# Layer a's transposed probabilities read back in a step of their own

## The chip, the cores and the metric

The kernel runs on one core of a Trainium2 chip. The metric is the time of one execution on the device in microseconds (us), the median of several runs.

## What is computed

A trunk of two residual layers on 256 tokens of width 2048, 16 heads of 128. Layer a is multi-head latent attention, layer b block-sparse attention with ALiBi (at 256 tokens: causal attention over one block). Cut to what matters for layer a:

```python
def mla_mixer(h, w_in, ...):
    q_lat, kv_lat, k_rope, gate = split(h @ w_in)
    q  = norm(q_lat) @ w_q_up      # per head 128 + 64 (rotary)
    kv = norm(kv_lat) @ w_kv_up    # per head k 128, v 128
    ...                            # RMS norm of q and k, rotary
    p = softmax(causal(q k^T * scale))
    return (p @ v) * silu(gate)
x = x + mla_mixer(rms_norm(x), ...) @ w_out_a
```

## The kernel before

**Matmuls.** A float32 product is made of three fast matmuls: every operand is split into a high part and a low part (`wh`, `wl` for weights, `ph`, `pl` for probabilities, `ohl` for the gated output). For each block of weights (512 KB, tile `wr`), ScalarE (ACT) makes `wh` (line 147), VectorE (DVE) makes `wl` (line 151), and TensorE (PE) uses both. Loads of weights go through SyncE's (SP's) queue, four blocks ahead.

**Layer a by pairs of heads.** `group_a(g)`, g = 0 to 7, does heads 2g and 2g+1, called pair g here. It projects q (`w_q_up`, blocks 384 wide) and k, v (`w_kv_up`, one block 512 wide), norms, and turns q, k and the rotary part by PE transposes in three steps, turn 0, 1, 2 (`ps_ta`; tiles `tok`, `tok`, `ra`), whose results ACT (`sf`, `sr`, lines 421 and 426) and DVE (`sr`, line 427) split. Blocks of the gate projection stand between a pair and the next.

**A head** has three steps (`head_steps`, line 450). `s1`: scores on PE (`ps_s`), then softmax on DVE and ACT, into `sm`. `s2`: the probabilities are transposed by a DMA: `fly` writes the two 16-bit halves of each float32 apart ("planes", line 441, on ACT in layer a) into `pz` and issues a DMA transpose from SP's queue (line 442) into `sm`; `flip` then copies the planes back together on DVE (line 448, `pz<-sm`). Then ACT makes `ph` (line 490) and `p` (line 493, in float32 for the second half) and DVE `pl` (line 491). `s3`: four matmuls with v (`ps_o`), the product with the gate `og` (DVE, line 505), its high part `ohl` (ACT, 506) and low part (DVE, 507).

**What sets the order.** `ordered` lays the main list (projections) and the side list (turns and heads) out on PE's planned time. A step becomes ready `lag * 1.3` ns after the steps that it needs; PE's order is fixed by that. The instructions of DVE, ACT and SP are then ordered by the framework's scheduler, by what becomes ready, each engine working its queue off in order. `head_steps` already has a second form, with `away`: `s2` only sends the planes off, and a further step `s2_back` copies them back (line 483, held at its place in the program by `keep_in_program_order`) and makes `ph`, `pl`, `p`. Layer b uses it (`FLB`, 4500 ns).

**The end of layer a.** The output projection `w_out_a` begins while the last pairs are still at work: four blocks of columns run through heads 0 to 11 first (48 PE steps of 0.67 us each), then through heads 12 to 15. Meanwhile SP reloads `x` (line 772) and layer b's distances into `c_sb` (line 768), from which ACT makes `alibi` (line 883).

Of the kernel before, what the change touches and what calls it, by code (L numbers as in the profile page):

```python
# [44 lines left out]


PA, PB, LO, TU, TUB, S1, S2A, S2B, S3 = 9000, 6000, 5000, 3000, 10000, 4800, 6000, 9000, 3000
FLB = 4500
SLACK = 1.3
HOLD = 4500  # L50
PACE, PACEB = 600, 3500
# [42 lines left out]
def trunk(ctx: ExitStack, tc, xT, gains, cst, w_in_a, w_q_up, w_kv_up, w_out_a, w_in_b, w_out_b, outT):  # L94
    nc = tc.nc
# [560 lines left out]
    def group_a(g):  # L656
# [65 lines left out]
        def scores(h):  # L722
            def f(ps):
                at = lambda x, i: [y[:, i] for y in x]
                products(ps, at(z["q"], h), at(z["k"], h), True)
                products(ps, at(z["r"], 0), at((krf,) + lat_st["kr"], h), False)
            return f
# [5 lines left out]
        for h in range(2):  # L733
            heads.append(head_steps(2 * g + h, scores(h), lambda: c_sb[:, C_MASK:C_MASK + 384],
                                    lambda h=h: [x[:, h] for x in z["v"]], 1090, turns + [kr], [], gates[g][-1:],
                                    S2A, nc.scalar.copy))
        proj[0].needs += lats
        if g > 1:
            proj[-1].after += turns_of[-2]
# [55 lines left out]
    for g in range(8):  # L795
        main += group_a(g)
        if g == 0:
            kr.after.append(main[-1])
        if g < 7:
            main += gates[g + 1][HALF:] + (gates[g + 2][:HALF] if g < 6 else [])  # L800
        gates[g][-1].after.append(row_a)
        if g > 3:
            gates[g][-1].after += [h[2] for h in heads[2 * g - 8:2 * g - 6]]
# [21 lines left out]
    def group_b(g):  # L825
# [49 lines left out]
        def scores(h):  # L875
            def f(ps):
                products(ps, [x[:, h] for x in z["Q"]], [x[:, h] for x in z["K"]], True)
            return f

        def bias(h):  # L880
            def f():
                b = wk.tile([P, 384], F32, tag="alibi", name="alibi", bufs=1)
                nc.scalar.activation(b, c_sb[:, C_MASK:C_MASK + 384], AF.Copy,
                                     scale=float(np.float32(2.0 ** (-8.0 * (h + 1) / H))))
                return b
            return f
# [12 lines left out]
        for h in range(4):  # L899
            hb.append(head_steps(4 * g + h, scores(h), bias(4 * g + h), lambda h=h: [x[:, h] for x in z["v"]],  # L900
                                 545, [tq, tk], v[-1:] + gate[-1:], [], S2B, nc.vector.tensor_copy, PACEB if g < 3 else PACE, FLB))
        for s in (gate[NC - 1], gate[-1]):
# [96 lines left out]
```

## Time and profile before

| | |
|---|---|
| median of 3 runs | 753.29 us (752.79, 753.29, 755.86) |
| profiled execution, its own time | 756.72 us |
| span in its trace | 754.9 us |
| PE, DVE, ACT busy | 99%, 78%, 65% of the span |
| DMA traffic | 153 MB, mean 203 GB/s |

Around the span lie 1.8 us (756.72 - 754.9). The matmuls' ends in a trace are modelled, so a wait of PE is read from the starts of successive matmuls: 256 columns follow one another every 0.11 us, 512 columns every 0.22 us.

### The profile page before, as it was taken

To read this page: it belongs to the slowest core of one execution; us is meant where nothing else is said; L and a number is where in the kernel's file an instruction comes from. 1 tells how busy PE (TensorE), PEld (TensorE's weight loads), DVE (VectorE), ACT (ScalarE), POOL (GpSimd) and SP (SyncE) were. 2 spreads that over 40 slices of the span, in tenths; PEclk is the share of its full clock that TensorE was granted. 3 is DMA by queue.
4 is the path that set the end of the run, shared out by engine and by line. 5 is a ranking of instruction groups with operands and counts; after the bars stand their busy time and mean duration, and the time that the engine had idled before them with its cause. 6 is when DMAs were issued, how large, how long until landed. Compare 5 with 4: busy or idle time off the path is not lost.

```text
span 754.9 us, 13198 instructions
## 1 busy us (share of the span) xinstructions
PE 743.7 (99%) x4766; PEld 692.0 (92%) x4766; DVE 589.7 (78%) x1244; ACT 492.1 (65%) x1041; POOL 0.2 (0%) x4
## 2 busy tenths in 40 slices
PE   8999999999999999999999999999999999999997
PEld 7999999999899999988889988898889988899997
DVE  6978899998898696875888967887787968878563
ACT  7867888887787475555666766666566756665441
POOL 0000000000000000000000000000000000000000
PEclk9999999999999999999999999999999999999999
DMA  9866666666566957667888868777778878767771
GB/s 294 265 182 182 167 184 162 182 172 158 161 195 170 299 172 227 198 191 200 222 230 208 203 195 234 224 195 208 197 235 226 197 204 228 230 197 196 248 223 49
DMA packets 150258, 153.13 MB, mean 203 GB/s; under 512 B 47280, under 2 KB 119344, under 8 KB 150192
## 3 DMA queue, kind: packets, MB, share of 16 engines
q1 hardware_dynamic: 150048, 152.27, 71.5%
q8 instruction: 37, 0.61, 0.3%
q14 instruction: 29, 0.24, 0.1%
q10 hardware_dynamic: 144, 0.02, 0.0%
HBM read 139.68 MB, written 2.10 MB: 188 GB/s over the span
## 4 chain that ended last, share of the span: by engine, by line
PE 89%; DVE 5%; DMA 3%; ACT 1%; issue 1%; SPq 0%; DVEq 0%; ACTq 0%
PE acc L199 82%; PE ps_s L199 4%; DVE wl L151 3%; PE ps_o L199 2%; PE ps_ta L202 1%; DMA c_sb<-cst 1%; DMA sm<-pz 1%; DMA wr<-w_in_a 1%; ACT wh L147 1%; DVE xt L406 0%; ACT sq L598 0%; DVE rs_y L328 0%; DVE rs_t L327 0%; PE ps_lt L202 0%; DVE pl L491 0%
## 5 line engine op out<-in xcount | busy, mean ns | idle before, releaser
L147 ACT ACTIVATE wh<-wr 128x1024 fp32r<-128x1024 f32 (+3 forms) x265 | 288.3, 1092 | 145.6 <-PE acc L199 118.9
L151 DVE TENSOR_TENSOR wl<-wr,wh 128x1024 fp32r<-128x1024 f32 (+3 forms) x265 | 313.9, 1188 | 74.1 <-PE acc L199 42.5
L199 PE MATMUL acc<-wh,xhl 128*128 128x512 f32 (+1 forms) x896 | 266.1, 376 | 1.5 <-ACT wh L147 1.5
L199 PEld LDWEIGHTS acc<-wh,xhl 128*128 128x128 f32 x896 | 169.1, 190 | 22.6 <-ACT wh L147 2.2
L199 PE MATMUL acc<-xhl,wh 128*128 128x256 f32 (+1 forms) x768 | 173.5, 313 | 0.0
L199 PE MATMUL acc<-ohl,wh 128*128 128x256 f32 (+1 forms) x800 | 172.5, 307 | 0.1
L199 PE MATMUL acc<-wl,xhl 128*128 128x512 f32 (+1 forms) x448 | 167.8, 374 | 0.8 <-DVE wl L151 0.8
L199 PE MATMUL acc<-ohl,wl 128*128 128x256 f32 x512 | 140.5, 274 | 0.4 <-DVE wl L151 0.3
L199 PE MATMUL acc<-xhl,wl 128*128 128x256 f32 x512 | 140.2, 274 | 0.0
L199 PEld LDWEIGHTS acc<-ohl,wh 128*128 128x128 f32 x800 | 130.1, 191 | 6.2 <-DVE ohl L507 0.3
L199 PEld LDWEIGHTS acc<-xhl,wh 128*128 128x128 f32 x768 | 126.3, 191 | 6.6
L199 PEld LDWEIGHTS acc<-ohl,wl 128*128 128x128 f32 x512 | 98.3, 192 | 0.9 <-DVE wl L151 0.8
L199 PEld LDWEIGHTS acc<-xhl,wl 128*128 128x128 f32 x512 | 98.2, 192 | 0.2
L199 PEld LDWEIGHTS acc<-wl,xhl 128*128 128x128 f32 x448 | 84.9, 190 | 11.3 <-DVE wl L151 1.3
L199 PE MATMUL acc<-wh,xt 128*128 128x384 f32 (+1 forms) x192 | 58.5, 362 | 0.0
L466 ACT ACTIVATE sm<-sm,mn 128x128 f32<-128x128 f32 x64 | 29.1, 456 | 12.8 <-DVE mn L464 12.8
L199 PEld LDWEIGHTS acc<-wh,xt 128*128 128x128 f32 x192 | 35.6, 192 | 1.4
L199 PE MATMUL acc<-wl,xt 128*128 128x384 f32 (+1 forms) x96 | 34.0, 354 | 2.1 <-DVE wl L151 2.1
L406 DVE TENSOR_TENSOR xt<-acc,xt 128x256 f32<-128x256 f32 (+1 forms) x37 | 16.1, 484 | 14.7 <-PE acc L199 14.7
L490 ACT CAST ph<-pz 128x256 fp32r<-128x256 f32 x32 | 12.9, 404 | 21.0 <-DVE pz L483 10.7
L507 DVE TENSOR_TENSOR ohl<-og,ohl 128x256 fp32r<-128x256 f32 x32 | 13.5, 424 | 12.0 <-ACT ohl L506 11.8
L506 ACT ACTIVATE ohl<-og 128x256 fp32r<-128x256 f32 x32 | 13.8, 435 | 13.5 <-DVE og L505 13.5
(150 smaller groups left out, 726.9 us busy)
## 6 DMA issues: line engine op xcount, KB each, us to landing
wr<-w_in_b SPq DMA_DIRECT2D x128, 512.0 KB, 4.0
wr<-w_in_a SPq DMA_DIRECT2D x32, 512.0 KB, 4.1
wr<-w_out_a SPq DMA_DIRECT2D x32, 512.0 KB, 4.5
wr<-w_out_b SPq DMA_DIRECT2D x32, 512.0 KB, 4.4
wr<-w_in_a SPq DMA_DIRECT2D x15, 416.0 KB, 5.2
wr<-w_q_up SPq DMA_DIRECT2D x16, 384.0 KB, 3.7
wr<-w_kv_up SPq DMA_DIRECT2D x8, 512.0 KB, 3.9
xt<-xT SPq DMA_DIRECT2D x4, 512.0 KB, 5.6
```

The lines of the kernel that those rows point to most:

```text
L147: nc.scalar.activation(self.ordering(self.h)[1], self.ordering(self.raw)[0], AF.Copy)
L151: nc.vector.tensor_tensor(self.ordering(self.l)[1], self.ordering(self.raw)[0], self.ordering(self.h.bitcast(F32))[1], op=ALU.subtract)
L199: chain(nc.tensor.matmul(*args, skip_group_check=True, **kw))
L202: chain(nc.tensor.transpose(*args))
L406: nc.vector.tensor_tensor(lines(y), unpaired(b[:, o:o + n]), lines(y), op=ALU.add)
L466: nc.scalar.activation(sm[:, sl], sm[:, sl], AF.Exp, bias=mn[:, t:t + 1], scale=-1.0, accum_out=rs[:, t:t + 1])
L490: nc.scalar.copy(ph, pz[:, :S])
L506: nc.scalar.activation(lines(ogh[:, h]), unpaired(og), AF.Copy)
L507: nc.vector.tensor_tensor(lines(ogl[:, h]), unpaired(og), lines(ogh[:, h].bitcast(F32)), op=ALU.subtract)
```

## The change

Layer a's heads take the second form: `head_steps` gets `away=FLA`, 4000 ns. The transposes go off in `s2`; the copy back and the making of `ph`, `pl` and `p` are a step of their own, planned 2000 ns (`S2A - FLA`) times 1.3 after that, so the sum of the lags up to `s3` stays 6000 ns times 1.3. The instructions are the same ones; the copy's line is 483 in place of 448.

```diff
-FLB = 4500
+FLA, FLB = 4000, 4500
...
-                                    S2A, nc.scalar.copy))
+                                    S2A, nc.scalar.copy, away=FLA))
```

What this does to the queues, at four places. First DVE, around the products of pair 0's turns (`sr`), before; the two copies and both `pl` stand above these rows:

```order
L394 TENSOR_TENSOR gx<-acc,rr_a 128x512
L491 TENSOR_TENSOR pl<-pz,ph 128x256
L151 TENSOR_TENSOR wl<-wr,wh 128x768
L396 SCALAR_TENSOR_TENSOR gate<-gate,gx 128x512
L427 SCALAR_TENSOR_TENSOR sr_1356<-ps_ta,gq_a,sr_1356 128x256
L427 SCALAR_TENSOR_TENSOR sr_1356<-ps_ta,g_sb,sr_1356 128x512
L427 SCALAR_TENSOR_TENSOR sr_1356<-ps_ta,sr_1356 128x128
L151 TENSOR_TENSOR wl<-wr,wh 128x1024 x2
L505 SCALAR_TENSOR_TENSOR og<-ps_o,gate 128x256
```

And the same place now:

```order
L427 SCALAR_TENSOR_TENSOR sr_1342<-ps_ta,gq_a,sr_1342 128x256
L427 SCALAR_TENSOR_TENSOR sr_1342<-ps_ta,g_sb,sr_1342 128x512
L483 COPY pz<-sm 128x2x384
L151 TENSOR_TENSOR wl<-wr,wh 128x1024
L427 SCALAR_TENSOR_TENSOR sr_1342<-ps_ta,sr_1342 128x128
L483 COPY pz<-sm 128x2x384
L491 TENSOR_TENSOR pl<-pz,ph 128x256
L151 TENSOR_TENSOR wl<-wr,wh 128x1024
L491 TENSOR_TENSOR pl<-pz,ph 128x256
L505 SCALAR_TENSOR_TENSOR og<-ps_o,gate 128x256
```

The first `wl` of 1024 columns here is that of `w_kv_up`. In pair 0 one copy stands ahead of it and both `pl` behind it. In pairs 1 to 4 the first copy stands between the first two `sr`, the first `pl` after the second `sr`, and the second copy and `pl` behind that `wl`, as in pair 2 now:

```order
L427 SCALAR_TENSOR_TENSOR sr_2038<-ps_ta,sr_2038 128x128
L151 TENSOR_TENSOR wl<-wr,wh 128x1024
L483 COPY pz<-sm 128x2x384
L151 TENSOR_TENSOR wl<-wr,wh 128x1024
L491 TENSOR_TENSOR pl<-pz,ph 128x256
L505 SCALAR_TENSOR_TENSOR og<-ps_o,gate 128x256
```

PE's order is the same up to pair 5. There turn 2 of pair 6 (`ra`) now stands ahead of the second head's `ps_o`, where before it came one half of `w_kv_up` later:

```order
L199 MATMUL acc<-wh,xt 128x512
L202 MATMUL ps_ta<-c_sb,ra 128x128 x2
L199 MATMUL ps_o<-ph,vh 128x256
L199 MATMUL ps_o<-pl,vh 128x256
L199 MATMUL ps_o<-ph,vl 128x256
L199 MATMUL ps_o<-p_3147,v_2524 128x128
```

ACT's queue at that place, now; `p_3147` is what the last matmul above reads, and `sf_3089<-ps_ta 128x128` reads turn 2's result. Before, this `ph` and `p` stood ahead of all of pair 6's `sf`:

```order
L668 ACTIVATE sqa,ga_st<-acc 128x64
L421 ACTIVATE sf_3089<-ps_ta 128x128
L666 ACTIVATE sqa,ga_st<-acc 128x128
L490 CAST ph<-pz 128x256
L668 ACTIVATE sqa,ga_st<-acc 128x64
L493 COPY p_3147<-pz 128x128
L666 ACTIVATE sqa,ga_st<-acc 128x128
L506 ACTIVATE ohl<-og 128x256
```

In the last pairs more moves: the scores of pair 6 come four PE steps earlier, its `ps_o` two and four steps earlier, and the two `ps_o` of pair 7 three steps later (after 44 and 48 steps of the output projection, before after 41 and 45). In ACT's queue `alibi` now stands ahead of the last head's `ohl`, before it stood behind it. SP's queue has the same instructions; the transposes of pairs 6 and 7 take other places between the loads.

## Rows read from the trace of the kernel before

**Rows 1.** The page's busy time by engine: busy us, share of the span, instructions.

```profile
PE 743.7 (99%) x4766; PEld 692.0 (92%) x4766; DVE 589.7 (78%) x1244; ACT 492.1 (65%) x1041; POOL 0.2 (0%) x4
```

**Rows 2.** The chain of waits over 80 to 260 us, in order of time: start us, length us, what. Shown are the second head's scores that follow pairs 2, 3 and 4, one piece on DVE, and the chain's end in the reload of `c_sb`.

```profile
152.71 1.16 PE ps_s L199 x10
...
168.72 1.14 DVE wl L151
...
174.98 1.16 PE ps_s L199 x10
...
200.66 1.16 PE ps_s L199 x10
...
255.65 7.74 DMA c_sb<-cst
```

**Rows 3.** PE's timeline in pair 3, around the two halves of `w_kv_up` (columns: start us, us, engine, line, operation, in brackets idle time before it and its releaser).

```profile
169.25 0.49 PE L199 MATMUL acc<-wh,xt 128*128 128x512 f32 x1
169.91 0.48 PE L199 MATMUL acc<-wl,xt 128*128 128x512 f32 x1 [0.17 <-DVE wl L151]
170.23 0.59 PE L199 MATMUL acc<-wh,xt 128*128 128x512 f32 x2
...
171.20 0.28 PE L199 MATMUL ps_o<-pl,vh 128*128 128x256 f32 x1
...
171.59 0.49 PE L199 MATMUL acc<-wh,xt 128*128 128x512 f32 x1
171.91 0.38 PE L199 MATMUL acc<-wl,xt 128*128 128x512 f32 x1
```

**Rows 4.** DVE's timeline in pair 3, from the second copy to the `wl` of `w_kv_up`.

```profile
165.49 0.61 DVE L448 COPY pz<-sm 128x768 uint16<-128x768 uint16 x1 [0.16 <-DMA sm<-pz]
...
166.62 0.42 DVE L491 TENSOR_TENSOR pl<-pz,ph 128x256 fp32r<-128x256 f32 x1
166.96 0.48 DVE L427 SCALAR_TENSOR_TENSOR sr<-ps_ta,gq_a,sr 128x256 fp32r<-128x256 f32 x1
167.77 0.75 DVE L427 SCALAR_TENSOR_TENSOR sr<-ps_ta,g_sb,sr 128x512 fp32r<-128x512 f32 x1 [0.33 <-ACT sr L426]
168.44 0.28 DVE L427 SCALAR_TENSOR_TENSOR sr<-ps_ta,sr 128x128 fp32r<-128x128 f32 x1
168.64 2.35 DVE L151 TENSOR_TENSOR wl<-wr,wh 128x1024 fp32r<-128x1024 f32 x2
```

**Rows 5.** Pair 4: DVE's second copy, from its timeline.

```profile
189.55 0.61 DVE L448 COPY pz<-sm 128x768 uint16<-128x768 uint16 x1 [1.97 <-DMA sm<-pz]
```

**Rows 6.** Pair 4: PE's timeline.

```profile
191.65 0.35 PE L199 MATMUL ps_o<-ph,vh 128*128 128x256 f32 x1 [0.47 <-DVE sr L427]
...
193.97 0.65 PE L199 MATMUL acc<-wl,xt 128*128 128x512 f32 x1 [1.26 <-DVE wl L151]
```

**Rows 7.** Busy time by stretch, 190 to 194 us and 194 to 198 us: length, PE, PEld, DVE, ACT, POOL busy (instructions), granted clock of PE as a share of full speed, DMA share, GB/s.

```profile
190.00:194.00 4.00, 2.27 (x15) 1.68 (x13) 3.67 (x8) 3.73 (x12) 0.00 (x0) 1.00 0.29 102
194.00:198.00 4.00, 4.00 (x13) 3.45 (x14) 2.31 (x5) 3.00 (x15) 0.00 (x0) 0.57 0.59 189
```

**Rows 8.** Pair 0: PE's timeline.

```profile
101.92 0.28 PE L199 MATMUL ps_o<-pl,vh 128*128 128x256 f32 x1
...
102.31 0.49 PE L199 MATMUL acc<-wh,xt 128*128 128x512 f32 x1
103.07 0.48 PE L199 MATMUL acc<-wl,xt 128*128 128x512 f32 x1 [0.27 <-DVE wl L151]
```

**Rows 9.** Pair 0: DVE's timeline, from the first copy to the second `sr`.

```profile
95.27 0.60 DVE L448 COPY pz<-sm 128x768 uint16<-128x768 uint16 x1
...
98.88 0.95 DVE L151 TENSOR_TENSOR wl<-wr,wh 128x768 fp32r<-128x768 f32 x1
99.75 0.69 DVE L396 SCALAR_TENSOR_TENSOR gate<-gate,gx 128x512 f32<-128x512 f32 x1
```

**Rows 10.** Pair 5: ACT's timeline, the second head's `ph` and `p`, an `sqa`, and the first `ohl`.

```profile
213.15 0.41 ACT L490 CAST ph<-pz 128x256 fp32r<-128x256 f32 x1
213.46 0.29 ACT L493 COPY p<-pz 128x128 f32<-128x128 f32 x1
...
215.31 0.29 ACT L666 ACTIVATE sqa<-acc 128x128 f32<-128x128 f32 x1
...
215.56 1.08 ACT L147 ACTIVATE wh<-wr 128x1024 fp32r<-128x1024 f32 x1
```

**Rows 11.** Pair 5: PE's timeline, the second head's `ps_o` and, later, turn 2.

```profile
216.38 0.27 PE L199 MATMUL ps_o<-ph,vh 128*128 128x256 f32 x1
...
218.28 0.38 PE L202 MATMUL ps_ta<-c_sb,ra 128*128 128x128 f32 x2
```

**Rows 12.** The end of layer a on ACT: the last head's `ohl` and `alibi`.

```profile
259.41 0.43 ACT L506 ACTIVATE ohl<-og 128x256 fp32r<-128x256 f32 x1
263.42 0.52 ACT L883 ACTIVATE alibi<-c_sb 128x384 f32<-128x384 f32 x1 [3.58 <-DMA c_sb<-cst]
```

**Rows 13.** The end of layer a on PE: two late `wl`.

```profile
252.22 0.39 PE L199 MATMUL acc<-ohl,wh 128*128 128x256 f32 x2
252.65 0.38 PE L199 MATMUL acc<-ohl,wl 128*128 128x256 f32 x1
...
275.79 0.38 PE L199 MATMUL acc<-ohl,wl 128*128 128x256 f32 x1 [0.31 <-DVE wl L151]
```

## The prediction

> **What bounds the kernel now.** First the page's busy time: PE is busy for 743.7 of 754.9 us, DVE 78%, ACT 65% [rows 1]. So nearly all of the time is matmuls that the change leaves as they are, and it can only win back or add waits of PE. Next the chain of waits over layer a [rows 2]: it runs on PE, with one piece of 1.14 us on DVE in each pair, the `wl` of `w_kv_up`. The reader should then look at PE's timeline there [rows 3]: the matmul with `wl` starts 0.66 us after the one with `wh` (169.25 to 169.91), while the same step half a block later takes 0.32 (171.59 to 171.91). That is 0.34 lost, and the next matmul loses 0.10 more (0.32 instead of 0.22): 0.45 us a pair.
>
> DVE's timeline says why `wl` is late [rows 4]. Ahead of it in DVE's queue stand the second head's copy, which waits 0.16 for its DMA, and its `pl`, and an `sr` that waits 0.33 for ACT. In pair 4 the DMA came much later, the copy stood 1.97 us [rows 5], PE stood 0.47 and 1.26 [rows 6], and then ran 4 us at a granted clock of 0.57, a mix of the levels 1.2 and 2.4 GHz [rows 7]. By the second head's scores that follow, that pair took 200.66 - 174.98 = 25.68 us where the one before took 174.98 - 152.71 = 22.27: 3.41 more [rows 2].
>
> **The sum's base.** The profiled execution took 756.72 us, 3.43 above the median of 753.29. The 3.41 of pair 4 are just that difference. My reading is that the median runs had a pair 4 like the others and the run of 755.86 had one like the profiled; the trace of one execution can't show it.
>
> **The change part by part.** No instruction is added, and DVE's and ACT's work stays the same; what counts is who stands behind whom.
>
> *Pair 4's accident* (-3.41). The second head's softmax now ends before the rotary work on DVE, so its planes leave earlier, and the copy is read after the `wl` of `w_kv_up` rather than before the gate. A DMA as late as that one no longer holds DVE. Bounds: -3.41 to 0; I take all of it, since nothing on the path to that `wl` waits for this DMA any more.
>
> *The late `wl` in pairs 1 to 4* (-1.4). Removed from ahead of it: the copy (0.50 from its start to the next), its wait 0.16, `pl` 0.34, and `sr`'s wait for ACT 0.33, which the first copy, now put between the two `sr`, fills. That is 1.33 us: `wl` ends near 168.5 where PE wants it at 169.57 (169.25 + 0.32). So the stall should go, 0.45 each. What is late next is the second `pl`: behind that `wl` come the copy 0.50, another `wl` 1.17 (half of the 2.35 of rows 4) and `pl` 0.34, so it ends near 170.5. PE, 0.45 earlier, wants it at 171.20 - 0.45 = 170.75 [rows 3]. That is a thin cover of 0.25 us, and DVE starts this stretch somewhat later than before, since it no longer gets PE's stall as a pause. So I count 0.35 a pair; bounds 0 and 0.45.
>
> *Pair 0* (+0.44). Here the order is worse: one copy stands ahead of the `wl` of `w_kv_up`, and the second copy ahead of both `pl`. I lay it out from 95.27, where the first copy stood [rows 9]: `wl`, the last rotary sum, the gate product, `wl` and `gate` take 0.87 + 0.33 + 0.60 + 0.87 + 0.60 and end at 98.5; the two `sr` end at 100.2, the second held by ACT, which splits the turns one after another; copy 0.50, `wl` 1.17, `sr` 0.20, copy 0.50 and `pl` 0.34 end at 102.9. PE wants the first `pl` at 101.92 [rows 8]: 0.98 lost at `ps_o`. Won back is the stall at `wl`, 103.07 - 102.31 - 0.32 + 0.10 = 0.54. Bounds: -0.54 (if DVE gets there in time) to +0.6.
>
> *Pair 5* (+1.35). Here PE's order itself changed: turn 2 stands directly ahead of the second `ps_o`, and on ACT that head's `ph` and `p` now stand behind `sf`, which reads turn 2. Before, they were done at 213.75, 2.6 us ahead of their use at 216.38 [rows 10, 11]. Now turn 2 starts there and ends 0.38 later, at 216.76. Then ACT, in its order: `sf` 0.16, `sqa` 0.25 (215.31 to 215.56), `ph` 0.31 (213.15 to 213.46), another `sqa` 0.2, `p` 0.29: about 218.0. DVE's `pl` needs `ph`, too, 0.42 on DVE, near 218.1. The four matmuls of `ps_o` would have reached `p` at 216.38 + 0.21 (two transposes) + 0.33 = 216.92; they reach it at 218.1 + 0.22 = 218.3. That is 1.35 to 1.4 of PE's time that no slack on DVE or in a DMA can take away, since the chain begins on PE itself. Bounds 0.9 (with `pl` not the last) and 1.6.
>
> *The end of layer a* (-0.7). Two late `wl` went with the copies' waits: the one at 252.65 cost 0.3 (two matmuls at 252.22 take 0.22, so it is 0.21 late, and the next one 0.10), the one at 275.79 about 0.5 (0.31 idle after a matmul of 0.38 that usually gives way after 0.22) [rows 13]. The loads that end in `c_sb` were held in SP's queue by DVE, which frees the buffers; freed DVE issues them earlier. I count -1.0 with what follows them. Against it, the last head's `ps_o` now comes 48 instead of 45 steps into the output projection and its `ohl` is read 51 steps in: 3 x 0.67 = 2.0 us instead of 4.0 for `og`, `ohl` high and low (about 1.4). On ACT `alibi` now stands ahead of that `ohl` and waits for `c_sb`. I count +0.3; the second rival has its price. Bounds -1.0 to +2.95.
>
> Sum: 756.72 - 3.41 - 1.4 + 0.44 + 1.35 - 0.7 = **753.0 us**. Against the median of 753.29 that is no change: less than 0.5% (3.77 us), about what a measurement of this kernel can tell.
>
> **A rule weighed.** In rows 7 PE's clock was whole while it stood for 1.73 of 4 us and 0.57 in the 4 us behind. The Trainium skill (TensorE: Matmul & The Clock Gate, HAM oscillation) says that idle stretches of PE throttle its clock, so that a stall is paid once more behind it. The trace agrees in pair 4, and shows no drop behind the 0.27 us of idle time in pair 0; it has no stall between, such as pair 5's. By the rule pair 5 would cost more than its stall; the third rival prices that from rows.
>
> **The rivals.**
>
> 1. *The new stalls are covered.* Pair 0's and pair 5's work gets through in time, all stalls at `wl` go: 756.72 - 3.41 - 0.54 - 4 x 0.45 - 1.0 = 750.0. For it: DVE is 78% busy, so it has room. Against it: the chain in pair 5 doesn't depend on DVE's room.
>
> 2. *The last `ohl` waits behind `alibi`* (the slower side). `c_sb` was issued at 255.65 and landed 7.74 later, at 263.39 [rows 2]; `alibi` followed at 263.42, and `ohl` had gone before, at 259.41 [rows 12]. If `c_sb` lands no earlier, `alibi` ends near 263.9, the two parts of `ohl` near 264.8. PE wants them at 51 steps. By the trace's clock, with pair 5's 1.35 added, that is about 261.85: 2.95 us of standing, and a clock drop like pair 4's behind it (4 us at 0.57: 4 x 0.43 = 1.7). Price 753.0 + 2.95 + 1.7 = 757.6. It decides from the point where `c_sb` lands after about 260.4. For it: the reload of `x`, which goes ahead of `c_sb`, must wait for the last scores, which now come later. Against it: DVE no longer stands for the last copy, and so the loads ahead of `c_sb` go out earlier.
>
> 3. *Pair 5's stall drops the clock.* 1.7 us more: 754.7.
>
> 4. *The waits only change places.* DVE is as loaded as before, so the stall at `wl` comes back at `pl` or the next pair: about the median, 753.3.
>
> **How the numbers follow.** The forecast (around 753.0, its own range 751.5 to 754.5) gets 0.47, the first rival 0.22, the second 0.16, the third 0.10, the fourth 0.05. The range must reach from the first rival to most of the second: 750.0 to 757.0. Faster by over 0.5% (under 749.5) needs the first rival and a little more than it counts, or repeats of the kernel before with pair 4's accident: 0.14. Slower by over 0.5% (over 757.1) needs the second rival, or clock drops in both pair 0 and pair 5: 0.18. The rest, 0.68, is no change.
>
> **What would show it.** In the new profile: no DMA among what DVE's copy waits for in layer a, and the second transposes of a pair issued about 3 us earlier; in pairs 1 to 4 the `wl` of `w_kv_up` done before PE wants it, and a pair's length near 21.9 us in place of 22.27; in pair 0 the wait at `ps_o`, for `pl`; in pair 5 a wait of over 1 us at the second `ps_o`, for ACT's `p` or DVE's `pl`; the granted clock behind it; in the last stretch `alibi`'s wait and where `ohl` comes. The prediction is wrong if pair 5 shows no stall, if pairs 1 to 4 keep theirs, or if the end of layer a stands for `c_sb`.

## The result, and the profile after

The changed kernel takes 758.60 us (median of 5 runs, 757.79 to 759.16) where the kernel before took 753.29. The medians lie 5.3 us apart; the ratio over the runs is 1.0056 (95% interval 1.0039 to 1.0073), which is 4.2 us. That is slower, by more than 0.5%, and 1.6 us above the end of the range. The profiled execution took 758.54 us, its span 756.7.

The page's busy times answer to [rows 1] and hardly differ; the work is the same.

```profile
PE 743.3 (98%) x4766; PEld 693.5 (92%) x4766; DVE 589.6 (78%) x1244; ACT 492.3 (65%) x1041; POOL 0.2 (0%) x4
```

The list of waits over 80 to 290 us of the changed kernel (who, on whom: us in total, times, longest) names three waits of PE that the kernel before did not have, and the wait of `alibi`:

```profile
ACT alibi L883 <- DMA c_sb<-cst: 2.4, 1, 2.4
...
PE ps_o L199 <- DVE pl L491: 1.8, 3, 0.8
PE acc L199 <- ACT ohl L506: 1.8, 1, 1.8
PE ps_o L199 <- ACT ph L490: 1.5, 1, 1.5
```

**Pairs 1 to 4 as forecast.** PE's timeline in pair 3 (compare [rows 3]): `wl` follows `wh` after 0.33 us instead of 0.66, and the second `pl` is there in time.

```profile
168.66 0.49 PE L199 MATMUL acc<-wh,xt 128*128 128x512 f32 x1
168.99 0.38 PE L199 MATMUL acc<-wl,xt 128*128 128x512 f32 x1
...
170.17 0.27 PE L199 MATMUL ps_o<-pl,vh 128*128 128x256 f32 x1
```

**Pair 0 as forecast.** PE stands at the first `pl` (compare [rows 8]): 1.12 us from the matmul before, where 0.11 is usual.

```profile
101.58 0.27 PE L199 MATMUL ps_o<-ph,vh 128*128 128x256 f32 x1
102.70 0.38 PE L199 MATMUL ps_o<-pl,vh 128*128 128x256 f32 x1 [0.85 <-DVE pl L491]
```

**Pair 5.** PE's timeline first (compare [rows 11]). The first `ps_o` stands too, and the second stands for `ph`:

```profile
209.58 0.27 PE L199 MATMUL ps_o<-ph,vh 128*128 128x256 f32 x1
210.20 0.38 PE L199 MATMUL ps_o<-pl,vh 128*128 128x256 f32 x1 [0.35 <-DVE pl L491]
...
212.10 0.38 PE L202 MATMUL ps_ta<-c_sb,ra 128*128 128x128 f32 x2
214.00 0.38 PE L199 MATMUL ps_o<-ph,vh 128*128 128x256 f32 x1 [1.52 <-ACT ph L490]
```

Turn 2 does stand directly ahead, as the prediction said, and PE wants `ph` behind it at 212.32 (212.10 + 0.22). On ACT (compare [rows 10]) `sf`, which reads turn 2, stands ahead of `ph`; but it began only at 213.13, 0.65 us after turn 2's end at 212.48. ACT had been at work with no pause over 0.03 us since the first head's `ph` at 208.80, and reached this `sf` no earlier.

```profile
208.80 0.41 ACT L490 CAST ph<-pz 128x256 fp32r<-128x256 f32 x1 [0.72 <-DVE pz L483]
...
211.21 1.08 ACT L147 ACTIVATE wh<-wr 128x1024 fp32r<-128x1024 f32 x1
...
213.13 0.27 ACT L421 ACTIVATE sf<-ps_ta 128x128 f32<-128x128 f32 x1
213.29 0.28 ACT L666 ACTIVATE sqa<-acc 128x128 f32<-128x128 f32 x1
...
213.54 0.41 ACT L490 CAST ph<-pz 128x256 fp32r<-128x256 f32 x1
```

On DVE the second copy, which `ph` reads, began only at 212.36 and ended at 212.95. That is late as well, but 0.59 us ahead of `ph`: the row of `ph` shows no wait for it.

```profile
210.57 1.22 DVE L151 TENSOR_TENSOR wl<-wr,wh 128x1024 fp32r<-128x1024 f32 x1
211.70 0.74 DVE L427 SCALAR_TENSOR_TENSOR sr<-ps_ta,g_sb,sr 128x512 fp32r<-128x512 f32 x1
212.36 0.59 DVE L483 COPY pz<-sm 128x768 uint16<-128x768 uint16 x1
```

**The end of layer a.** On ACT (compare [rows 12]) `alibi` waits for `c_sb`, and `ohl` waits behind it, though `og` had been written from 258.56 on:

```profile
260.85 0.52 ACT L883 ACTIVATE alibi<-c_sb 128x384 f32<-128x384 f32 x1 [2.44 <-DMA c_sb<-cst]
261.28 0.41 ACT L506 ACTIVATE ohl<-og 128x256 fp32r<-128x256 f32 x1
```

PE stands for it, and runs on at a lower granted clock (0.78 and 0.79 in the two stretches behind; a mix of 2.4 and 1.2 GHz). That costs (0.22 + 0.21) x 4 = 1.7 us more, as in [rows 7]:

```profile
259.72 0.28 PE L199 MATMUL acc<-ohl,wl 128*128 128x256 f32 x1
261.74 1.04 PE L199 MATMUL acc<-ohl,wh 128*128 128x256 f32 x2 [1.75 <-ACT ohl L506]
```

```profile
260.00:264.00 4.00, 2.17 (x9) 1.99 (x10) 0.75 (x2) 1.33 (x3) 0.00 (x0) 0.78 0.48 157
264.00:268.00 4.00, 4.00 (x31) 4.00 (x30) 3.26 (x7) 2.58 (x5) 0.00 (x0) 0.79 0.35 100
```

**A ledger of layer a.** To compare executions I cut PE's time at seven matmuls that every version runs: the 193rd, 257th and 449th `acc<-xhl,wh` (94.81, 117.16, 184.01 us in the trace of before), the 11th `ps_o<-ph,vh` (214.48), and the 41st, 121st and 361st `acc<-ohl,wh` (227.51, 245.52, 304.50). Each number is the length of a piece less the shortest that any execution here has: what is lost there, in us. A star marks a piece that holds a clock drop of 1.7. What lies ahead of 94.81 differs by up to 2.3 us between these executions (0.9 between the two of the kernel before), where the change does nothing, and is left out.

| | pair 0 | pairs 1-3 | pair 4 | pair 5 | pair 6 | end |
|---|---|---|---|---|---|---|
| before (the profile shown) | 0.0 | 1.4 | 3.9* | 0.0 | 0.0 | 0.9 |
| before_again | 0.1 | 1.4 | 0.5 | 0.1 | 0.6 | 2.7 |
| after | 0.6 | 0.0 | 0.0 | 2.8 | 1.2 | 4.0* |
| after_again | 0.6 | 0.0 | 0.0 | 4.4* | 0.7 | 2.4 |
| alibi_behind | 0.6 | 0.0 | 0.0 | 4.4* | 1.2 | 0.1 |
| pair5_alone | 0.0 | 1.4 | 0.5 | 2.7 | 1.6 | 4.5* |
| all_but_pair5 | 0.6 | 0.0 | 0.0 | 1.8 | 2.0 | 0.0 |
| pairs1to4 | 0.2 | 0.0 | 0.0 | 2.2 | 1.8 | 1.1 |
| turn2_held | 0.6 | 0.0 | 0.0 | 4.6* | 0.2 | 0.0 |
| pairs1to7_turn2 | 0.1 | 0.1 | 0.0 | 4.9* | 0.4 | 0.0 |
| load_behind | 0.2 | 1.0 | 0.0 | 0.8 | 1.6 | 1.2 |
| pair5_2000 | 0.4 | 0.1 | 0.0 | 0.4 | 0.3 | 0.0 |
| pair5_2500 | 0.0 | 0.6 | 0.0 | 1.4 | 0.0 | 0.0 |

### The profile page after: what moved, and what is told of

It reads as the page before. It is cut to its first block, busy times and chain, and to the rows that moved or that the text cites. A ratio compares the mean times of both kernels' runs of the same rounds, so it can differ in the third digit from the quotient of the medians.

```text
span 756.7 us, 13200 instructions
## 1 busy us (share of the span) xinstructions
PE 743.3 (98%) x4766; PEld 693.5 (92%) x4766; DVE 589.6 (78%) x1244; ACT 492.3 (65%) x1041; POOL 0.2 (0%) x4
## 4 chain that ended last, share of the span: by engine, by line
PE 64%; DVE 1%; issue 0%
PE acc L199 61%; PE ps_o L199 1%; PE ps_s L199 1%; DVE wl L151 0%; PE ps_r L199 0%; DVE xt L406 0%; DVE rs_t L326 0%; DVE rs_y L328 0%; DVE rs_t L327 0%; DVE ohl L507 0%; DVE diag L370 0%; DVE rs_y L324 0%; DVE rs_y L323 0%; DVE rv_b L361 0%; DVE rx L787 0%
## 5 line engine op out<-in xcount | busy, mean ns | idle before, releaser
L199 PEld LDWEIGHTS acc<-ohl,wh 128*128 128x128 f32 x800 | 131.7, 193 | 8.1 <-ACT ohl L506 1.9
```

The source lines that it names most:

```text
L199: chain(nc.tensor.matmul(*args, skip_group_check=True, **kw))
```

## The experiments

**alibi_behind.** One order put back:

```diff
-            nc.scalar.activation(lines(ogh[:, h]), unpaired(og), AF.Copy)
+            tails.append(nc.scalar.activation(lines(ogh[:, h]), unpaired(og), AF.Copy))
...
-                nc.scalar.activation(b, c_sb[:, C_MASK:C_MASK + 384], AF.Copy,
+                ins = nc.scalar.activation(b, c_sb[:, C_MASK:C_MASK + 384], AF.Copy,
...
+                if h == 0:
+                    after(ins, tails[15])
```

> The changed kernel with one order put back: on ACT the first `alibi` comes behind the last head's `ohl`. Theory (the end of layer a stands because `ohl` is queued behind an `alibi` that waits for `c_sb`): the stall of 1.75 us at 259.72 and the lower clock behind it (0.78 and 0.79 in 8 us, some 1.8 us) go, so 758.6 - 3.5 = about 755. Rival (the last `ps_o` was put three PE steps later, and its `ohl` is late by itself, or the clock falls for another reason): 757.5 to 758.6.

Measured: 756.17 us where before ran at 754.48 beside it; ratio 1.0024 (1.0012 to 1.0036). ACT's timeline: `ohl` goes first, and now only `alibi` waits.

```profile
260.58 0.45 ACT L506 ACTIVATE ohl<-og 128x256 fp32r<-128x256 f32 x1 [0.56 <-DVE og L505]
263.04 0.52 ACT L883 ACTIVATE alibi<-c_sb 128x384 f32<-128x384 f32 x1 [2.01 <-DMA c_sb<-cst]
```

The end loses 0.1 instead of 4.0 or 2.4, so the order on ACT was the cause there. How much time that gives back is less sure: by the ratios (1.0056 to 1.0024) some 2.4 us, by the medians (5.3 to 1.7 us above the kernel before) 3.6, where 3.5 was expected. In the profiled execution the clock dropped behind pair 5 instead (granted 0.63 in 214 to 218 us; 4.4* in the ledger).

**pair5_alone** and **all_but_pair5**. The new form for pair 5 only, and for all others:

```diff
-                                    S2A, nc.scalar.copy, away=FLA))
+                                    S2A, nc.scalar.copy, away=FLA if g == 5 else 0))
```

```diff
-                                    S2A, nc.scalar.copy, away=FLA))
+                                    S2A, nc.scalar.copy, away=FLA if g != 5 else 0))
```

> The kernel before with the new form for pair 5 alone. PE's order is that of the changed kernel, and `alibi` stands ahead of the last `ohl`. Theory (all that the change loses at pair 5, pair 6 and the end comes from pair 5's steps): 753.3 + 2.7 (pair 5) + 1.2 (pair 6) + 3.1 (the end, net) = about 760. Rival (pair 6's stall and the end's need the new form in pairs 6 and 7 too): 753.3 + 2.7 = 756, or less.

Measured: 762.84 us, ratio 1.0117 (1.0098 to 1.0135), even more than counted. The profiled execution has two clock drops, one at the start and one at the end. Pair 5, pair 6 and the end lose about what the changed kernel loses there (2.7, 1.6 and 4.5*). Pair 5's second transpose landed here after 2.8 us, at 211.17, and the copy began only at 215.23, so a late landing is not needed for pair 5's stall. `alibi` is again the wait at the end:

```profile
264.61 0.52 ACT L883 ACTIVATE alibi<-c_sb 128x384 f32<-128x384 f32 x1 [2.94 <-DMA c_sb<-cst]
265.04 0.41 ACT L506 ACTIVATE ohl<-og 128x256 fp32r<-128x256 f32 x1
```

> The changed kernel with the first form for pair 5 alone. PE's order is that of the kernel before, and `ohl` comes ahead of `alibi`. Theory: 753.3 + 0.6 (pair 0) - 1.8 (pairs 1 to 4) = about 752.1, less if the late `wl` at the end go. Rival (the copies of pairs 6 and 7 at their place in the program hold DVE by themselves): 754 or more, with DVE's waits in pairs 6 and 7.

Measured: 755.04 us, ratio 1.0015 (0.9998 to 1.0032): about as before, not 2 us faster. The end is clean, pairs 1 to 4 win their 1.4 + 0.5, and pair 5 loses 1.8 although it has the form of before. The rival's number came true, but not its cause as it stands: pair 6 does lose 2.0, and pairs1to4, next, loses 1.8 there without the new form in pairs 6 and 7.

**pairs1to4.** The new form for four pairs:

```diff
-                                    S2A, nc.scalar.copy, away=FLA))
+                                    S2A, nc.scalar.copy, away=FLA if 0 < g < 5 else 0))
```

> The new form for pairs 1 to 4 alone. Theory (the late `wl` is what the form wins, 0.45 a pair): 753.3 - 1.8 = about 751.5, and pair 0 and pairs 5 to 7 as before. Rival (what is won in pairs 1 to 4 is given back by a late product in pairs 5 to 7 or at the end): 753.

Measured: 755.40 us, ratio 1.0020 (1.0006 to 1.0033). The rival holds: what pairs 1 to 4 win is given back in pairs 5 and 6. DVE's second copy of pair 5 waits as pair 4's did in [rows 5], and PE (second fence) waits for what stands behind it:

```profile
209.61 0.61 DVE L448 COPY pz<-sm 128x768 uint16<-128x768 uint16 x1 [1.78 <-DMA sm<-pz]
```

```profile
212.37 0.48 PE L199 MATMUL acc<-wl,xt 128*128 128x512 f32 x1 [0.93 <-DVE wl L151]
...
214.50 0.38 PE L199 MATMUL ps_o<-ph,vh 128*128 128x256 f32 x1 [0.78 <-DVE sr L427]
```

In the trace its transpose left SP at 203.56, 0.57 us behind a load of 512 KB, and landed 6.0 us later. Pair 5's second transpose in the kernel before left long after a load (209.66, the load at 205.79) and landed after 2.8.

**before_again.** The kernel before, unchanged.

> The kernel before, profiled once more. Theory (a late transpose in pair 4 is an accident of one execution, and the common run has none): pair 4 takes as long as pair 3 (22.3 us by the second head's scores that follow), pairs 5 and 6 run through without a wait of PE over 0.3 us, and the time is near 753.3 or, with a clock drop at some other place, near 755. Rival (the waits only change places: without pair 4's stall, PE stands in pairs 5 and 6, as in the run of the new form for pairs 1 to 4): 1 to 2 us of waits in each of pairs 5 and 6.

Measured: 754.78 us in one execution. The accident of pair 4 is not there: the copy waits 0.24 instead of 1.97 [rows 5], and PE's row at the `wl` of pair 4 is like pair 3's.

```profile
187.03 0.61 DVE L448 COPY pz<-sm 128x768 uint16<-128x768 uint16 x1 [0.24 <-DMA sm<-pz]
```

```profile
191.45 0.48 PE L199 MATMUL acc<-wl,xt 128*128 128x512 f32 x1 [0.24 <-DVE wl L151]
```

Pair 4 is 3.4 us shorter (3.9 to 0.5 in the ledger), pair 5 loses nothing (0.1), and pair 6 only 0.6. But the time is not near 753.3, though the clock stayed whole in layer a: the end loses 2.7 where the first profile has 0.9, at four late `wl`, of which this is the last:

```profile
273.98 0.38 PE L199 MATMUL acc<-ohl,wl 128*128 128x256 f32 x1 [0.31 <-DVE wl L151]
```

That is the rival in part: waits moved, to the end and not to pair 5. So the kernel before, with or without its accident, does not lose in pair 5 what pairs1to4 does.

**turn2_held** and **pairs1to7_turn2**. Turn 2 of pair 6 waits in the plan for pair 5's second `ps_o`; the second kernel has pair 0 in the first form, too.

```diff
+        if g == 6:
+            turns[2].after += [heads[11][2]]
         proj[0].needs += lats
```

> The changed kernel with one order put back: turn 2 of pair 6 waits in the plan for the second head's `ps_o` of pair 5. PE's whole order is then that of the kernel before, and `ohl` comes ahead of `alibi`. Theory (turn 2's new place is what costs at pair 5 and at the end): against the kernel before + 0.6 (pair 0) - 1.8 (pairs 1 to 4) + 1.5 (pair 6), that is +0.3, 754.8 where before is 754.5; pair 5 without a wait over 0.4. Rival (the second transpose of pair 5, sent right behind a load, lands 6 us later and holds pair 5 in any form): 1.8 more, 756.6.

> The same, with pair 0 in the first form. Theory: 0.6 less than with pair 0, 754.2 where before is 754.5. Rival: 756.0.

Measured: 754.88 us, 1.0015 (1.0001 to 1.0028), and 755.37, 1.0014 (1.0002 to 1.0026), where before ran at 753.57. The end is clean (0.0), since `ohl` now goes ahead of `alibi`; pair 6 loses less. The times lie between the two: +1.1 us against before by the ratios, where the theory has +0.3 and -0.3 and the rival +2.1 and +1.5. Pair 5 decides it against the theory, and not as the rival has it either: with turn 2 moved away PE still stands for `ph`, 4.6 less the clock's 1.7 = 2.9 us in all. Here are DVE's timeline of turn2_held, ACT's, and PE's row:

```profile
210.30 1.22 DVE L151 TENSOR_TENSOR wl<-wr,wh 128x1024 fp32r<-128x1024 f32 x1
211.43 0.74 DVE L427 SCALAR_TENSOR_TENSOR sr<-ps_ta,g_sb,sr 128x512 fp32r<-128x512 f32 x1
212.09 0.59 DVE L483 COPY pz<-sm 128x768 uint16<-128x768 uint16 x1
...
213.68 0.43 DVE L491 TENSOR_TENSOR pl<-pz,ph 128x256 fp32r<-128x256 f32 x1 [0.70 <-ACT ph L490]
```

```profile
212.99 0.28 ACT L666 ACTIVATE sqa<-acc 128x128 f32<-128x128 f32 x1
...
213.26 0.39 ACT L490 CAST ph<-pz 128x256 fp32r<-128x256 f32 x1
```

```profile
213.71 0.38 PE L199 MATMUL ps_o<-ph,vh 128*128 128x256 f32 x1 [1.72 <-ACT ph L490]
```

The transpose left at 202.13 and landed 6.2 us later, at 208.3. The copy began at 212.09, not waiting for anything: it stood at its place in the program, behind a `wl` and an `sr`, 3.8 us after its data. PE wants `ph` at 211.61 + 0.22 = 211.83. The copy ended at 212.68, and `ph` began 0.58 later, behind `wh` and four `sqa` on ACT, which again had worked without a pause since the first head's `ph` (208.53). So two queues were late for PE: ACT's by most, DVE's less. An estimate from these rows: a `ph` right behind the copy (0.09 later, as in pair5_2000 below) would have let PE go on at 213.2, so 1.4 of the 1.9 us would have stayed; with the copy earlier and `ph` in its place on ACT, all of it. Pair 0's form (0.6 or 0.1 in the ledger) is not to be seen in the times.

**load_behind.** pairs1to4, with the load that stood between pair 5's two transposes put behind the second (`sent` holds the transposes in their order, the eleventh and twelfth are pair 5's):

```diff
+            loads.append(ins)
+            if len(loads) == 75:
+                after(ins, sent[11])
```

> The new form for pairs 1 to 4 alone (755.4 before this edit), with the load of `w_out_a` that stands in SP's queue between pair 5's two transposes put behind the second. Theory (that transpose takes 6.0 us because it goes off right behind a load, and DVE's copy, with `wl` behind it, waits for it): it lands about 3 to 3.5 us after its issue, pair 5's 2.2 us go, 753.2. Rival (it is slow because the first transpose went off 1.9 us earlier, or because of the loads already under way): still 4.5 to 6 us and about 755.4.

Measured: 754.73 us, 1.0011 (0.9996 to 1.0027). The time from issue to landing (shortest, median, longest): the second transpose of pair 5 in pairs1to4, and both of the pair here (the second is the 3.7).

```profile
DMA to landing us min/median/max: 6.0/6.0/6.0
```

```profile
DMA to landing us min/median/max: 3.7/4.0/4.4
```

The second copy no longer waits, and pair 5 loses 0.8 instead of 2.2. So this transpose landed later for the load just ahead of it. The first transpose now takes 4.4 us where it took 2.7, and the first copy waits 0.34 for it; why is not shown. By all runs' time alone (753.2 expected, 754.7 measured, the intervals overlapping) this would not be settled; the landing and the ledger show it. Of the runs with a mean granted clock of 0.999 or 1.0, seven of either, the medians are 753.31 here and 755.35 in pairs1to4, where the kernel before beside them had 753.41 and 753.29. In this execution pairs 1 to 3 lose 1.0, mostly at one second `pl` of pair 2.

**pair5_2000** and **pair5_2500**. pairs1to7_turn2 with another `away` for pair 5, 2000 (below) or 2500:

```diff
-                                    S2A, nc.scalar.copy, away=FLA))
+                                    S2A, nc.scalar.copy, away=0 if g == 0 else 2000 if g == 5 else FLA))
```

> Turn 2 held as before this, pair 0 in the first form, and for pair 5 alone `away` 2000 ns in place of 4000, which moves its two copies up in DVE's queue: the first stands right behind the last rotary sum, the second ahead of the second `wl` instead of behind three more instructions. PE's order is that of the kernel before. Theory (pair 5 lost 2.9 us and a clock drop because its second copy, kept at its place in the program, began at 212.1 though its transpose had landed at 208.3): the copy starts near 208.4, no wait of PE over 0.3 us in pair 5, the clock stays whole there. By segments against the second profile of the kernel before: -1.4 (pairs 1 to 3), -0.5 (pair 4), 0 (pair 5), -0.4 (pair 6), -2.6 (the end), at most -4.9; counted -3, some 750.7 where before is 753.6. Rival (the late landing itself, 6.2 us after the issue, is what holds pair 5): the copy waits for its DMA and the `wl` behind it comes late, 1 to 2 us lost, 752.5 or more.

> The same with 2500 ns for pair 5: both copies stand together behind the gate product, ahead of a `wl`, and both `pl` behind that. Theory (DVE's order decides): copies from 207.8 to 208.9, `wl` to 210.0, first `pl` to 210.4, where the first `ps_o` wants it at 209.4; so the first `ps_o` stands 1.0, the second not at all; 1.0 slower than with 2000. Rival: as with 2000, or 2 us lost at the second `ps_o` as with 4000.

Measured: 751.79 us, 0.9971 (0.9957 to 0.9986), and 751.39, 0.9958 (0.9940 to 0.9976), before at 753.88: faster than both kernels, by 2.1 and 2.5 us against the kernel before, where some 3 and 2 were counted. DVE's second copy with 2000 ns, `ph` on ACT, and PE's second `ps_o`, 0.53 us after the matmul before it (210.84) instead of 0.22:

```profile
208.80 0.59 DVE L483 COPY pz<-sm 128x768 uint16<-128x768 uint16 x1
```

```profile
209.48 0.41 ACT L490 CAST ph<-pz 128x256 fp32r<-128x256 f32 x1 [0.34 <-DVE pz L483]
```

```profile
211.37 0.35 PE L199 MATMUL ps_o<-ph,vh 128*128 128x256 f32 x1
```

With 2500 ns both copies, `wl` and both `pl` came at the expected times to 0.2 us, and the wait moved to the first `ps_o`, as expected:

```profile
208.01 1.15 DVE L483 COPY pz<-sm 128x768 uint16<-128x768 uint16 x2
209.05 1.21 DVE L151 TENSOR_TENSOR wl<-wr,wh 128x1024 fp32r<-128x1024 f32 x1
210.18 0.75 DVE L491 TENSOR_TENSOR pl<-pz,ph 128x256 fp32r<-128x256 f32 x2
```

```profile
210.65 0.38 PE L199 MATMUL ps_o<-pl,vh 128*128 128x256 f32 x1 [1.12 <-DVE pl L491]
```

The transposes land as late as before (6.0 and 6.2 us), so the landing is not what held pair 5 in the changed kernel; the place of the copy-back step is. The edit moves the step as a whole: with the copy on DVE, `ph` on ACT went ahead of the `wh` and the `sqa` that it stood behind, and now waits for the copy. No run moves one of the two alone; that ACT's queue held more is read from the rows of turn2_held. That 2500 is 1.0 slower than 2000 holds in pair 5 (1.4 against 0.4 in the ledger), but the times don't bear it out: they are the same within their intervals.

**after_again.** The changed kernel, unchanged.

> The changed kernel once more. If the segments read from one execution are those of every execution: pair 0 +0.6, pair 5 +2.7, pair 6 +1.2 and the end +3 against the kernel before, with a clock drop behind the wait at the end; 758 where before is 753.6. If some were chance, their segment will differ by over 1 us.

Measured: 757.95 us, ratio 1.0056 (1.0037 to 1.0074), as the first time. Pair 0, pair 5 less the clock (2.7) and the stall at the end come again; the clock drop lies behind pair 5 this time, and the end, without it, loses 2.4.

## Why the prediction failed, point by point

Two steps of the sum failed, pair 5's and the end's. By the first profile the end's is the larger.

- *Pair 4's accident* (-3.41): right. before_again and pair5_alone have a pair 4 that is shorter by 3.4, and no version with the new form there has the accident. The reading that it alone parted the profiled execution from the median was too simple: before_again took 754.78 without it, 1.2 above the median of 753.57 beside it, with 2.7 lost at the end.
- *The late `wl`* (-1.4): right in mechanism, 1.4 + 0.5 = 1.9 won; the pairs take 21.83 us where some 21.9 was forecast. The thin cover at the second `pl` held in most executions; in load_behind it did not.
- *Pair 0* (+0.44): right, 0.6, at the `pl` named.
- *Pair 5* (+1.35): this step failed. It cost 2.7 to 2.9 and, in some executions, a clock drop. The forecast had `ph` and `p` late because they stand behind turn 2 and its `sf` on ACT, and let `sf` begin when turn 2 ends. That ACT still had other work then, and began `sf` 0.65 us later, was left out. So was the first `ps_o`, which stood for `pl` and lost 0.5 (210.20 - 209.58 - 0.11). turn2_held shows that the stall stays without turn 2, so turn 2 was not the cause. The two last kernels show that it goes when the copy-back step comes earlier: the step, planned 4000 ns behind the transposes, came late in DVE's queue and in ACT's, and `ph` last, behind `wh` and `sqa`. The prediction asked which instructions that read turn 2 stood ahead of `ph`, and not how far ACT and DVE would be when PE got there.
- *The end* (-0.7): this step failed, too, in its +0.3 for `ohl` behind `alibi`; the second rival came true, and with it the prediction's own sign of being wrong, that the end of layer a stands for `c_sb`. The rival's condition was `c_sb` landing after 260.4; the row of `alibi` puts it at about 260.8. It priced the stall at 2.95 and the clock at 1.7; the trace has 1.75 idle and 1.7. It had a chance of 0.16 because DVE was to free the loads earlier. That it did: `c_sb` was issued at 253.16 instead of 255.65. But PE, too, wanted `ohl` earlier, at 259.83 (259.72 + 0.11) where the prediction had 261.85, so 2.0 of the 2.5 us gained were gone. alibi_behind shows the cause. Against the first profile of before the end lost 3.1 more; against before_again, with its four late `wl`, only 1.3, and after_again without the clock drop no more at all.
- *Pair 6*: not in the sum. 0.7 to 1.2 lost at its `ps_o`, which the plan had put two and four steps earlier, with DVE's copy waiting 0.7 for its DMA, though no such wait was to be left in layer a. Holding turn 2, which brings PE's order back, leaves 0.2 and 0.4.
- *The rule weighed*: by the Trainium skill (TensorE: Matmul & The Clock Gate, HAM oscillation) idle stretches of PE throttle its clock, so that a stall is paid again. The trace agrees behind the end's stall in the first profile. It doesn't in after_again: there the granted clock stayed 1.00 in 260 to 264 us, though PE was busy for only 2.10 of the 4, and had been 0.81 and 0.76 in the 8 us behind 212. The third rival (a drop behind pair 5) so came true in some executions and not in others.

The sum of the errors, by the ledger against the profile of before: pair 5 1.4 more (2.75 for 1.35), the end 3.8 more (+3.1 for -0.7), pair 6 1.2, pair 0 0.15, less 0.5 in pairs 1 to 4, makes 6.0; what lies ahead of pair 0 and behind the end was 0.5 shorter. 758.6 - 753.0 is 5.6.

What stays open: why pair 6 loses 1.6 to 2.0 in the three versions in which pair 5 keeps the first form and earlier pairs have the new one. Their traces show pair 6's first transpose landing after 4.4 to 4.6 us, and DVE's copy waiting 1.3 to 1.65 for it, where it took 3.4 in the kernel before; yet it leaves 1.3 us behind a load in all of them. That was not tried by itself, and neither was the copy or `ph` of pair 5 alone. Why the clock drops behind one stall and not behind another is not shown either.

## What to carry to other kernels

A step that is put off by a fixed delay must be checked against its consumer in every repetition of a loop, above all in the last ones, where the neighbours differ, and on every engine that it uses: the same 4000 ns that won 0.46 us a pair in pairs 1 to 4 lost 2.7 in pair 5, where ACT was the last to get to it. Where a queue's order flips in front of an instruction that waits for a DMA, price it by the landing, and ask whether the consumer will come earlier, too. And an edit that removes a wait lets everything behind it come earlier, transfers included, which then meet other transfers.

## What was not expected of the hardware

- The same transpose (128 x 384 words) landed 2.7 to 2.8 us after its issue when the last load had gone off some 4 us before (4.5 in pair 4's accident), and 5.9 to 6.4 when it left some 0.6 us behind a load of 512 KB (second transposes of pairs 2 and 5 where the pairs ahead have the new form; 4.3 to 4.8 in pairs 0, 3 and 4, so a load just ahead is not all of it). Pair 5's, in pairs1to4, left 2.8 us earlier by PE's clock than in before_again and landed 0.4 us later. The Trainium skill (DMA: Bandwidth & Descriptors, Queues, rings and completion order) says that each DMA engine takes the descriptors of a queue in ring order; load_behind agrees with it for that transpose, 3.7 us with the load behind; the 4.4 of the first it leaves open.
- A clock drop cost about 1.7 us wherever it came in these traces, and it came at different places in executions of one kernel: pair 4 in one profile of the kernel before and nowhere in layer a in the other; at the start (around 11 to 15 us) in four of the other profiles. Of 29 runs of the kernel before on one chip, those with a mean granted clock of 0.999 or 1.0 took 752.0 to 755.0, those below 754.5 to 756.7. So one profile's difference of 1.7 us proves nothing until the granted clock is compared.
